# A hybrid attention layer: the stick-breaking mask moves into the running product, keys are stacked by DMA, and top-k steps are spread by other weights

## The chip, the cores and the metric

The kernel runs on one core of a Trainium2 chip. Its engines are TensorE (PE, matmuls, with PEld loading weights), VectorE (DVE), ScalarE (ACT), GpSimd (POOL) and SyncE (SP, which issues all DMA transfers here). The metric is device time in microseconds, the median of several runs; a profile is one execution with the hardware profiler on.

## What is computed

One decoder layer over T = 1040 positions (16 meta tokens and 1024 of the sequence), width 1024. One input projection gives the queries, keys and values of two attention branches, their gates, and an indexer. Cut to what matters here:

```python
# branch a: stick-breaking, 8 heads of 64
z = q @ k.T * 64 ** -0.5
mask = key_pos < q_pos                                   # strictly causal
log_beta = log_sigmoid(z)
log_1m = where(mask, log_beta - z, 0)
suffix = reverse_cumsum(log_1m) - log_1m
a = where(mask, exp(log_beta + suffix), 0);  y_a = a @ v
# branch b: every query attends to the 256 best keys of the indexer
score = where(causal, sum_h(relu(qi_h @ ki.T) * wi_h), -inf)
idx = top_k(score, 256)                                  # ties: the earlier key
y_b = softmax(q @ k[idx].T * 64 ** -0.5 + rel_bias) @ v[idx]
# both: gates, two projections, an output projection, residual, layer norm
```

## The kernel before

The sequence is stored in reverse, so that the suffix sum is a running product from left to right: with 1 - sigmoid(z) = sigmoid(-z), the scan of sigmoid(-z) over the keys gives the products, and differences of the values (dv) replace differences of the products. Products of float matrices are made from a high part and a low part (hi and lo) in three or two matmuls.

Work comes in stages: layer norm and the first projections, the indexer's scores, branch a (about 203 to 691 us), branch b, and the tail with the output projections. Branch a has 32 units: 4 groups m of two heads h, and 4 pairs pr of blocks of 128 queries. Its loop (lines 1081 to 1096) weaves, unit by unit, five generators: `stick_scores` of the next unit (977), `stick_values` of this one (1018), the projections of the next group and the gates (`projections`, 334), and two feeds of top-k steps. PE's instructions are pinned to the order in which they are written; the other engines' order is set by a scheduler that follows program order as far as buffers and its own estimates allow. Operations of the top-k feeds are "behind" (934): they follow the stage's own last operation and nothing of the stage waits for their place.

Scores: `qk` (476) multiplies a block of 128 queries with chunks of the stacked keys, hi and lo of the query; in the first chunk of each of the 8 blocks of a head a third product, of an identity and the tile `not_before`, adds -30000 where a key is not yet allowed. ACT takes sigmoid(-z) into `ct`, DVE scans it in place (989).

Keys: `k_item` (382) projects 128 columns, which are two heads, in three chunks of 348, 346 and 346. Per head, ACT copies 64 rows into rows 0 to 63 of the tile `sk`, and DVE writes what the copy's rounding left out into rows 64 to 127. The projection's PSUM tag `pj` has two banks. For branch b's keys (one head) `extra` copies the values from the same bank, after the keys.

Top-k: for 7 blocks, j = 0 to 6, of width 1040 - 128j, the 256th best score is found bit by bit, 15 steps on the high 16 bits of the scores, 16 on the low ones. DVE does blocks 2 to 6 (`step`, 820: five counts and three small operations), ACT and POOL do blocks 0 and 1 (`act_topk`, 855) with sums of signs into a junk tile with the one-buffer tag `sca`. Between the halves, `low_half` (828) loads the scores again from DRAM, into the one-buffer tag `se`. After the last bit `topk` (914) runs what is left of ACT's steps (920), forms the thresholds of all blocks and calls `select` (894) for each: load the scores into `se`, count, mark the equal ones, rank them by a scan into a tile with tag `sca`, and write the mask through POOL. A generator's `yield` tells its cost to the weaving; here each step counts 1:

```python
    TOPK_OPS = 33 * (NK - len(AB)) + 3 * NK
    ACT_OPS = 34 * len(AB)
    spare = [max(0.5, TK_SLOT - stick_busy(i)) for i in range(TK_END)] + [0.0] * (len(units) - TK_END)
    n_tk = (TOPK_OPS + 1) * spare[i] / sum(spare)
    n_at = ACT_OPS / AT_END
```

DVE's top-k budget is thus spread over the first 30 units, ACT's over the first 26. `keep_y` (950) splits a finished output of a branch into two halves of one tile on POOL and stores both with one transfer.

Of the kernel before, what the change touches and what calls it, by code (L numbers as in the profile page):

```python
# [49 lines left out]
TK_END, TK_SLOT, TK_FILL = 30, 16.0, 3.0  # L50
# [6 lines left out]
AB, AT_END = (0, 1), 26  # L57
# [111 lines left out]
def layer_kernel(ctx: ExitStack, tc: tile.TileContext, x, meta, g_col, b_col, g_row, b_row, rel,  # L169
# [306 lines left out]
    def qk(j, c0, n, q2, sk, mask=None):  # L476
# [4 lines left out]
        if mask is not None:  # L481
            mm(p[:, mask:mask + 128], ident_h, not_before, start=False, stop=False)
# [21 lines left out]
    wsc = cst.tile([128, NB, 8], F32, name="wsc")  # L504
    m9 = cst.tile([128, 9], F32, name="m9")
    v9 = cst.tile([128, 9], F32, name="v9")
# [215 lines left out]
    ski = idxp.tile([128, T], F32R, name="ski")  # L722
    sc = idxp.tile([128, off(NB)], F32, name="sc")
# [104 lines left out]
    def low_half(j):  # L828

        st = sbt([128, T], F32, "se", "st")  # L830
        SY.dma_start(st[:, :width(j)], sc_d[:, span(j)])
        yield 1
        lw = sbt([128, T], U16, "scr", "lw")
        l16 = st.bitcast(U16).rearrange("p (n two) -> p n two", two=2)[:, :width(j), 0]
        V.tensor_scalar(lw[:, :width(j)], l16, sgn[:, j:j + 1], lofs[:, j:j + 1], op0=ALU.mult, op1=ALU.add)
        V.scalar_tensor_tensor(yk[:, span(j)], xk[:, span(j)], top[:, j:j + 1], lw[:, :width(j)],
                               op0=ALU.is_equal, op1=ALU.mult)
# [17 lines left out]
    def act_topk():  # L855
# [5 lines left out]
        def steps(keys, bits):  # L861
            for b in bits:
                for j in AB:
# [5 lines left out]
                    yield 1  # L869
# [6 lines left out]
        for j in AB:  # L876
# [16 lines left out]

    def select(j):
# [11 lines left out]
        yield 1  # L906
# [5 lines left out]
        yield 1  # L912

    def topk():
# [13 lines left out]
        for j in range(NK - 1, -1, -1):  # L928
            yield from select(j)
# [522 lines left out]
```

## Time and profile before

| | us |
|---|---|
| median of 3 runs | 1080.26 (1079.41 to 1080.92) |
| the profiled execution, its own time | 1082.33 |
| its span, first to last instruction | 1079.2 |
| PE / DVE / ACT / POOL busy | 1023.9 / 800.7 / 554.7 / 406.6 |
| mean granted clock of TensorE | 0.983 |

All times in the rows are microseconds from the start of the span unless marked ns. In a row of a timeline the first two numbers are the start and the length; `out<-in` are the program's tile names; a bracket tells the idle time of that engine before the instruction, and what ended it. L218 and L228 are helpers through which all operations of DVE and ACT, and all matmuls, pass. "pj" is a projection's bank, "z" a bank of scores, "atr" and "vtr" transposes, "pv" weighted values, "st" and "s" reloaded scores, "lw" a low half, "scr" the counts' junk output. A row of a stretch has its ends, its length, the busy time of PE, PEld, DVE, ACT and POOL with their instructions, the mean granted clock (1.00 is 2.4 GHz), the DMA engines' share and GB/s. A row of a group ends with its count, busy us, mean ns of one, and the engine's idle time before it; a row of waits with us in total, times and the longest; a row of DMA issues with count, KB each and median us from issue to landing.

### The profile page before, as it was taken

How to read it: one execution, taken by the hardware profiler on the slowest of the kernel's cores; microseconds unless marked ns; L12 is line 12 of the kernel's file. 1: busy time of each engine (PE TensorE's matmuls, PEld its weight loads, DVE VectorE, ACT ScalarE, POOL GpSimd, SP SyncE). 2: the span in 40 equal slices, each digit the busy share in tenths (PEclk: the TensorE clock that was granted, in tenths of full speed). 3: DMA queues.
4: the chain of work that ended last, by engine and by line, in shares of the span. 5: the costliest groups of instructions: out<-in, count | busy, mean ns of one | idle time of the engine just before them, and what ended most of it. 6: DMA issues, size and time to landing. Idle time of an engine off the chain costs nothing.

```text
span 1079.2 us, 16973 instructions
## 1 busy us (share of the span) xinstructions
PE 1023.9 (95%) x5659; PEld 877.5 (81%) x5659; DVE 800.7 (74%) x1721; ACT 554.7 (51%) x1223; POOL 406.6 (38%) x542
## 2 busy tenths in 40 slices
PE   4989999999999998999999989999999999999997
PEld 3878889887888897888888877888888888877886
DVE  7845778787878797878878788277777787277755
ACT  4615566565666555665665343366666765145000
POOL 4312111344354445543544426543535341263000
PEclk8989999999999998999999999999999999999999
DMA  7543655315222433315122534442525853787311
GB/s 278 196 130 89 147 123 157 116 57 152 66 98 84 118 109 105 123 64 137 55 93 94 151 96 131 157 122 82 142 70 130 302 164 127 251 275 258 122 40 58
DMA packets 77255, 142.15 MB, mean 132 GB/s; under 512 B 9400, under 2 KB 28600, under 8 KB 77040
## 3 DMA queue, kind: packets, MB, share of 16 engines
q1 hardware_dynamic: 77168, 141.08, 42.6%
q8 instruction: 44, 0.72, 0.3%
q14 instruction: 43, 0.35, 0.1%
HBM read 78.38 MB, written 39.65 MB: 109 GB/s over the span
## 4 chain that ended last, share of the span: by engine, by line
PE 72%; DVE 14%; DMA 6%; issue 3%; ACT 3%; POOL 1%; SPq 0%; DVEq 0%; ACTq 0%; POOLq 0%
PE pj L228 36%; PE z L228 9%; PE po L228 8%; PE pv L228 7%; PE br L228 5%; PE ptr L231 3%; PE atr L231 3%; DVE scr L218 2%; DMA s<-sc_d 2%; DVE ct L218 2%; DVE hT L218 2%; DVE rank L218 1%; DMA wraw<-in_w_o_dram 1%; DMA st<-sc_d 1%; DVE e L218 1%
## 5 line engine op out<-in xcount | busy, mean ns | idle before, releaser
L228 PE MATMUL pj<-hT,whi 128*128 128x512 f32 (+4 forms) x1680 | 503.8, 382 | 15.7 <-DVE sk L218 6.5
L228 PEld LDWEIGHTS pj<-hT,whi 128*128 128x128 f32 x1680 | 286.5, 193 | 43.3 <-DVE hT L218 7.3
L228 PE MATMUL pj<-hT,wlo 128*128 128x512 f32 (+4 forms) x840 | 312.4, 372 | 0.0
L316 POOL TENSOR_TENSOR wlo<-wraw,whi 128x512 fp32r<-128x512 f32 x108 | 149.0, 1381 | 189.8 <-ACT whi L218 173.3
L228 PEld LDWEIGHTS pj<-hT,wlo 128*128 128x128 f32 x840 | 161.9, 193 | 24.2
L218 DVE TENSOR_SCALAR_CACHE_REDUCE scr<-mk_all,cand 128x784 bf16<-128x784 int16 (+9 forms) x160 | 120.9, 755 | 2.3
L228 PE MATMUL z<-sk,sq 128*128 128x272 f32 (+3 forms) x448 | 120.5, 344 | 1.5 <-ACT ct L218 1.0
L218 ACT ACTIVATE whi<-wraw 128x512 fp32r<-128x512 f32 x108 | 67.8, 629 | 66.4 <-PE pj L228 41.4
L218 DVE TENSOR_TENSOR_SCAN ct<-ct 128x1040 f32<-128x1040 f32 (+3 forms) x64 | 96.4, 1507 | 4.3 <-ACT ct L218 4.1
L228 PEld LDWEIGHTS z<-sk,sq 128*128 128x128 f32 x448 | 78.7, 191 | 12.9 <-DVE mxs L218 2.9
L228 PE MATMUL po<-wo,M 128*128 128x512 f32 (+1 forms) x408 | 88.8, 379 | 0.0
L228 PEld LDWEIGHTS po<-wo,M 128*128 128x128 f32 x408 | 73.3, 188 | 15.6 <-DVE gt L218 0.6
L228 PE MATMUL br<-yh,whi 128*128 128x512 f32 x256 | 82.0, 401 | 2.6 <-DVE gt L218 2.6
L1129 POOL TENSOR_TENSOR mb<-mk_all,nbt 128x256 f32<-128x256 bf16 (+3 forms) x64 | 46.5, 730 | 81.8 <-DVE mxs L218 77.3
L218 ACT ACTIVATE ct<-z 128x272 f32<-128x272 f32 (+3 forms) x112 | 50.4, 452 | 41.9 <-PE z L228 38.4
L218 ACT ACTIVATE sca<-mk_all,ncand 128x1040 bf16<-128x1040 int16 (+1 forms) x64 | 70.8, 1107 | 0.5
L218 DVE TENSOR_TENSOR atlo<-atr,athi 128x512 fp32r<-128x512 f32 x80 | 54.7, 686 | 21.5 <-ACT athi L218 15.9
L866 POOL TENSOR_SCALAR dn<-sg,need 128x1 f32<-128x1 f32 x62 | 23.6, 380 | 122.8 <-ACT sca L218 121.7
L218 DVE SCALAR_TENSOR_TENSOR sc<-r,wsc,sc 128x272 f32<-128x272 f32 (+4 forms) x98 | 57.2, 609 | 14.8 <-ACT r L218 14.0
L218 ACT ACTIVATE r<-z 128x272 f32<-128x272 f32 (+4 forms) x112 | 49.2, 452 | 35.2 <-PE z L228 29.0
L218 ACT ACTIVATE athi<-ptr 128x512 fp32r<-128x512 f32 (+1 forms) x96 | 52.9, 558 | 26.4 <-PE ptr L231 24.8
L218 DVE TENSOR_TENSOR atlo<-ptr,athi 128x512 fp32r<-128x512 f32 (+1 forms) x96 | 61.1, 644 | 6.2 <-ACT athi L218 3.2
(205 smaller groups left out, 1750.1 us busy)
## 6 DMA issues: line engine op xcount, KB each, us to landing
sq<-aq SPq DMA_DIRECT2D x96, 256.0 KB, 4.0
wraw<-in_w_in_dram SPq DMA_DIRECT2D x92, 256.0 KB, 2.9
g_d<-gs SPq DMA_DIRECT2D x34, 256.0 KB, 2.2
gt<-g_d SPq DMA_DIRECT2D x32, 256.0 KB, 3.6
xn_d<-xt SPq DMA_DIRECT2D x8, 512.0 KB, 3.6
xr<-xn_d SPq DMA_DIRECT2D x32, 128.0 KB, 2.3
res_d<-xr SPq DMA_DIRECT2D x32, 128.0 KB, 1.8
ya_d<-yl SPq DMA_DIRECT2D x16, 256.0 KB, 2.8
```

Of the source, the lines that this page charges most:

```text
L218: ins = getattr(self.engine, op)(*args, **kw)
L228: pin(nc.tensor.matmul(*args, **kw))
L231: pin(nc.tensor.transpose(*args))
L316: last_lo[0] = G.tensor_tensor(lo, raw, f(hi), ALU.subtract).ins.name
L866: G.tensor_scalar(dn[:, c], sg[:, c], need2[:, c], -(2.0 ** b), op0=ALU.is_ge, op1=ALU.mult)
L1129: G.tensor_tensor(mb[:, :n], mk[:, :n], NBT[m][:, h, :n], ALU.add)
```

## The change

The mask product and its two constant tiles go. The scan takes a second tensor, `not_yet`, which is 1 where a key is not yet allowed and 0 elsewhere, and keeps the larger of product and mask, so the running product stays 1 up to the first allowed key. With two heads, `k_item` copies all 128 rows into a tile `ak` of the tag `A`, subtracts once, and sends the four quarters to the two `sk` tiles by DMA; `extra` now comes first. The top-k generators yield estimated times in place of 1. `low_half` becomes one generator over several blocks that loads the next block as soon as the present one's low half is extracted. `topk` selects blocks 6 to 2 first, and only then runs the rest of ACT's steps, forms the thresholds of blocks 0 and 1, and selects these. The two budgets are spread over 32 and 28 units. `keep_y` writes the low part in place and stores in two transfers. The tiles `wsc`, `m9`, `v9` move to the indexer's pool.

```diff
-TK_END, TK_SLOT, TK_FILL = 30, 16.0, 3.0
+TK_END, TK_SLOT, TK_FILL = 32, 16.0, 3.0
-AB, AT_END = (0, 1), 26
+AB, AT_END = (0, 1), 28
...
-    ident_h = cst.tile([128, 128], BF16, name="ident_h")
-    V.tensor_copy(ident_h, ident)
-    not_before = cst.tile([128, 128], BF16, name="not_before")
-    V.memset(not_before, -30000.0)
-    G.affine_select(not_before, not_before, [[-1, 128]], ALU.is_ge, 0.0, base=0, channel_multiplier=1)
...
             cs = slice(c0, c0 + n)
+            if extra:
+                extra(ci, c0, n, p)
+            if len(rows) == 2:
+                a = sbt([128, 2, 348], F32R, "A", "ak")
+                A.activation(a[:, 0, :n], p[:, :n], AF.Copy)
+                V.tensor_tensor(a[:, 1, :n], p[:, :n], f(a[:, 0, :n]), ALU.subtract)
+                for t, r in zip(SK[key], rows):
+                    for i in range(2):
+                        SY.dma_start(f(t[64 * i:64 * i + 64, cs]), f(a[r:r + 64, i, :n]))
+                return
             for t, r in zip(SK[key], rows):
                 A.activation(t[0:64, cs], p[r:r + 64, :n], AF.Copy)
                 V.tensor_tensor(t[64:128, cs], p[r:r + 64, :n], f(t[0:64, cs]), ALU.subtract)
-            if extra:
-                extra(ci, c0, n, p)
...
         mm(p[:, :n], q2[:, 0, qs], sk[:, c0:c0 + n], start=True, stop=False)
-        if mask is not None:
-            mm(p[:, mask:mask + 128], ident_h, not_before, start=False, stop=False)
         mm(p[:, :n], q2[:, 1, qs], sk[:, c0:c0 + n], start=False, stop=True)
...
+    LOAD, LW, YK, EQ, RANK = 1.0, 0.0015, 0.002, 0.0017, 0.0031
+    def count_cost(j):
+        return 0.2 + width(j) / 925
...
-            yield 1
+            yield count_cost(j)
...
+    def low_half(blocks):
+        def load(j):
+            st = sbt([128, T], F32, "se", "st")
+            SY.dma_start(st[:, :width(j)], sc_d[:, span(j)])
+            return st
+        st = load(blocks[0])
+        yield LOAD
+        for j, j1 in zip(blocks, blocks[1:] + [None]):
+            lw = sbt([128, T], U16, "scr", "lw")
+            l16 = st.bitcast(U16).rearrange("p (n two) -> p n two", two=2)[:, :width(j), 0]
+            V.tensor_scalar(lw[:, :width(j)], l16, sgn[:, j:j + 1], lofs[:, j:j + 1], op0=ALU.mult, op1=ALU.add)
+            if j1 is not None:
+                st = load(j1)
+            yield LW * width(j)
+            V.scalar_tensor_tensor(yk[:, span(j)], xk[:, span(j)], top[:, j:j + 1], lw[:, :width(j)],
+                                   op0=ALU.is_equal, op1=ALU.mult)
+            yield YK * width(j)
...
-        yield 1
+        yield LOAD
         t_ = f(thr)
         count(s[:, :w], t_, j)
         V.tensor_scalar(cnt[:, j:j + 1], cnt[:, j:j + 1], -float(TOPK), None, op0=ALU.add)
+        yield count_cost(j)
         e = sbt([128, T], I16, "scr", "e")
         r = sbt([128, T], I16, "sca", "rank")
         V.tensor_scalar(e[:, :w], s[:, :w], t_[:, j:j + 1], None, op0=ALU.is_equal)
+        yield EQ * w
         V.tensor_tensor_scan(r[:, :w], e[:, :w], e[:, :w], 0.0, ALU.add, ALU.max)
-        yield 1
+        yield RANK * w
         V.scalar_tensor_tensor(r[:, :w], r[:, :w], cnt[:, j:j + 1], e[:, :w], op0=ALU.is_le, op1=ALU.mult)
+        yield RANK * w
         V.scalar_tensor_tensor(e[:, :w], s[:, :w], t_[:, j:j + 1], r[:, :w], op0=ALU.is_ge, op1=ALU.subtract)
+        yield EQ * w
...
-        run(at.rest())
-        V.tensor_copy(thr, top)
...
+        threshold(vs)
         s = mk_all[:, span(NB - 1)]
         V.memset(s, 0.0)
         causal_mask(s)
-        for j in range(NK - 1, -1, -1):
+        for j in range(NK - 1, len(AB) - 1, -1):
+            yield from select(j)
+        run(at.rest())
+        threshold(slice(0, len(AB)))
+        for j in AB[::-1]:
             yield from select(j)
...
+    TOPK_OPS = (32 * sum(map(count_cost, rest)) + sum(map(count_cost, range(NK))) + (NK + 1) * LOAD
+                + sum((LW + YK) * width(j) for j in rest) + sum(2 * (EQ + RANK) * width(j) for j in range(NK)))
+    ACT_OPS = 32 * sum(map(count_cost, AB)) + LOAD + sum((LW + YK) * width(j) for j in AB)
...
-        G.tensor_copy(t[:, 0], y)
-        G.tensor_tensor(t[:, 1], y, f(t[:, 0]), ALU.subtract)
-        SY.dma_start(dst, f(t))
+        G.tensor_copy(t, y)
+        G.tensor_tensor(y.bitcast(F32R), y, f(t), ALU.subtract)
+        SY.dma_start(dst[:, 0], f(t))
+        SY.dma_start(dst[:, 1], y)
+    not_yet = stkp.tile([128, T], BF16, name="not_yet")
+    V.memset(not_yet, 0.0)
+    V.memset(not_yet[:, 0:128], 1.0)
+    G.affine_select(not_yet[:, 0:128], not_yet[:, 0:128], [[-1, 128]], ALU.is_ge, 0.0, base=0, channel_multiplier=1)
...
-            V.tensor_tensor_scan(b, b, b, 1.0, ALU.mult, ALU.min)
+            V.tensor_tensor_scan(b, b, not_yet[:, :w], 1.0, ALU.mult, ALU.max)
```

## Rows read from the trace of the kernel before

**Rows 1.** The page, busy time of each engine, share, instructions.

```profile
PE 1023.9 (95%) x5659; PEld 877.5 (81%) x5659; DVE 800.7 (74%) x1721; ACT 554.7 (51%) x1223; POOL 406.6 (38%) x542
```

**Rows 2.** Stretches of the stick-breaking stage (columns as told above).

```profile
251.90:301.60 49.70, 45.12 (x278) 41.62 (x276) 38.38 (x78) 29.47 (x67) 22.61 (x34) 0.97 0.35 99
301.60:385.30 83.70, 83.44 (x460) 70.80 (x460) 67.73 (x148) 52.15 (x112) 40.15 (x67) 1.00 0.35 105
385.30:437.00 51.70, 44.60 (x269) 40.36 (x267) 45.11 (x84) 28.35 (x66) 24.67 (x30) 0.93 0.34 100
...
506.80:566.60 59.80, 56.83 (x340) 50.30 (x338) 47.95 (x105) 38.36 (x87) 28.65 (x47) 1.00 0.24 78
566.60:691.00 124.40, 117.95 (x639) 99.45 (x638) 94.11 (x157) 49.91 (x110) 56.90 (x64) 0.99 0.39 117
```

**Rows 3.** Timeline of PE, a masked chunk, then one of the later branch.

```profile
385.16 0.29 PE L228 MATMUL z<-sk,sq 128*128 128x272 f32 x1
...
385.54 0.27 PE L231 MATMUL atr<-ident,ct 128*128 128x128 f32 x1
...
701.74 0.41 PE L228 MATMUL z<-sk,sq 128*128 128x272 f32 x2
701.99 0.27 PE L231 MATMUL pv<-ident,smb 128*128 128x128 f32 x1
```

**Rows 4.** Groups by form on DVE, 190 to 690: two scans.

```profile
L218 DVE TENSOR_TENSOR_SCAN ct<-ct 128x912 f32<-128x912 f32 x8 | 16.4, 2054 | 0.1
...
L218 DVE TENSOR_TENSOR_SCAN rank<-e 128x912 int16<-128x912 int16 x1 | 2.0, 2027 | 0.0
```

**Rows 5.** Timelines of DVE and ACT, one key chunk.

```profile
271.53 0.51 DVE L218 TENSOR_TENSOR sk<-pj,sk 64x348 fp32r<-64x348 f32 x1
272.56 0.52 DVE L218 TENSOR_TENSOR sk<-pj,sk 64x348 fp32r<-64x348 f32 x1 [0.52 <-ACT sk L218]
...
272.08 0.46 ACT L218 ACTIVATE sk<-pj 64x348 fp32r<-64x348 f32 x1 [6.52 <-DVE sk L218]
```

**Rows 6.** Waits of ACT and PE, 190 to 692.

```profile
ACT sk L218 <- DVE sk L218: 24.2, 7, 6.5
ACT vtb L218 <- DVE sk L218: 10.6, 3, 4.2
...
PE pj L228 <- DVE sk L218: 6.5, 6, 2.0
...
PE pj L228 <- ACT vtb L218: 2.5, 1, 2.5
```

**Rows 7.** Groups by form on ACT, 190 to 690: a 128-row copy.

```profile
L218 ACT ACTIVATE kv<-pj 128x348 f32<-128x348 f32 x3 | 1.4, 453 | 0.0
```

**Rows 8.** DMA issues, the queries' transfers.

```profile
sq<-aq SPq DMA_DIRECT2D x96, 256.0 KB, 4.0
```

**Rows 9.** Timelines of SP, DVE, PE at the low halves; one load's issue.

```profile
407.00 8.64 SPq L831 DMA_DIRECT2D st<-sc_d  x3
...
410.83 0.69 DVE L218 TENSOR_SCALAR lw<-st,sgn,lofs 128x784 uint16<-128x784 uint16 x1 [2.75 <-DMA st<-sc_d]
...
423.00 1.11 PE L231 MATMUL vtr<-ident,dv 128*128 128x128 f32 x4 [5.38 <-DVE at L218]
...
st<-sc_d SPq DMA_DIRECT2D x1, 392.0 KB, 3.7
```

**Rows 10.** The page, the group of all counts on DVE.

```profile
L218 DVE TENSOR_SCALAR_CACHE_REDUCE scr<-mk_all,cand 128x784 bf16<-128x784 int16 (+9 forms) x160 | 120.9, 755 | 2.3
```

**Rows 11.** Timeline of DVE, first and last use of rank in two selections.

```profile
633.98 2.32 DVE L218 TENSOR_TENSOR_SCAN rank<-e 128x656 int16<-128x656 int16 x1
...
639.98 0.89 DVE L218 SCALAR_TENSOR_TENSOR e<-s,thr,rank 128x656 int16<-128x656 f32 x1
...
647.13 2.24 DVE L218 TENSOR_TENSOR_SCAN rank<-e 128x784 int16<-128x784 int16 x1
...
650.57 1.30 DVE L218 SCALAR_TENSOR_TENSOR e<-s,thr,rank 128x784 int16<-128x784 f32 x1
```

More of the change, by code (lines that the diff above doesn't have):

```diff
@@ L474, in zb_item, with qk @@
         return Z_B + m, Q_CH, evac, None
-    def qk(j, c0, n, q2, sk, mask=None):
+    def qk(j, c0, n, q2, sk):
         p = pst("z", "z")
@@ L503, in layer_kernel @@
     ki = {}
-    wsc = cst.tile([128, NB, 8], F32, name="wsc")
-    m9 = cst.tile([128, 9], F32, name="m9")
-    v9 = cst.tile([128, 9], F32, name="v9")
     def ki_evac(ci, c0, n, p):
@@ L722, in layer_kernel @@
     ski = idxp.tile([128, T], F32R, name="ski")
+    wsc = idxp.tile([128, NB, 8], F32, name="wsc")
+    m9 = idxp.tile([128, 9], F32, name="m9")
+    v9 = idxp.tile([128, 9], F32, name="v9")
     sc = idxp.tile([128, off(NB)], F32, name="sc")
@@ L826, in step @@
         V.tensor_scalar(cand[:, vs], cand[:, vs], -(2.0 ** (b - 1) if b else 1.0), None, op0=ALU.add)
-    def low_half(j):
-        st = sbt([128, T], F32, "se", "st")
-        SY.dma_start(st[:, :width(j)], sc_d[:, span(j)])
-        yield 1
[L833 to L837, printed above, removed]
+    def low_half(blocks):
[15 more added lines that the diff above has]
+            yield YK * width(j)
     def low_halves():
@@ L843, in low_halves @@
             count(xk[:, span(j)], cand, j)
-            yield 1
+            yield count_cost(j)
         V.tensor_tensor(need[:, vs], need[:, vs], cnt[:, vs], ALU.subtract)
-        for j in range(len(AB), NK):
-            yield from low_half(j)
+        yield from low_half(list(range(len(AB), NK)))
         V.memset(cand[:, vs], float(1 << 15))
@@ L868, in steps @@
                                     op0=ALU.add, op1=ALU.add)
-                    yield 1
+                    yield count_cost(j)
         G.memset(ncand, 0.5 - (1 << 14))
@@ L881, in act_topk @@
             G.tensor_scalar(need2[:, c], need2[:, c], sg[:, c], -float(width(j)), op0=ALU.subtract, op1=ALU.add)
-            yield 1
-        for j in AB:
-            yield from low_half(j)
+            yield count_cost(j)
+        yield from low_half(list(AB))
         G.memset(ncand, 0.5 - (1 << 15))
@@ L892, in causal_mask, with threshold @@
         G.affine_select(s[:, 0:128], s[:, 0:128], [[1, 128]], ALU.is_ge, -BIG, base=0, channel_multiplier=-1)
+    def threshold(c):
+        V.tensor_copy(thr[:, c], top[:, c])
+        V.tensor_copy(thl[:, c], cand[:, c])
+        V.scalar_tensor_tensor(thr[:, c], thr[:, c], 16, thl[:, c], op0=ALU.logical_shift_left, op1=ALU.bitwise_or)
+        V.tensor_tensor(thr[:, c], thr[:, c], rowm[:, c], ALU.bitwise_xor)
     def select(j):
@@ L901, in select @@
         V.tensor_scalar(cnt[:, j:j + 1], cnt[:, j:j + 1], -float(TOPK), None, op0=ALU.add)
+        yield count_cost(j)
         e = sbt([128, T], I16, "scr", "e")
@@ L927, in topk @@
         causal_mask(s)
-        for j in range(NK - 1, -1, -1):
+        for j in range(NK - 1, len(AB) - 1, -1):
             yield from select(j)
-    TOPK_OPS = 33 * (NK - len(AB)) + 3 * NK
-    ACT_OPS = 34 * len(AB)
+        run(at.rest())
+        threshold(slice(0, len(AB)))
+        for j in AB[::-1]:
+            yield from select(j)
+    rest = range(len(AB), NK)
+    TOPK_OPS = (32 * sum(map(count_cost, rest)) + sum(map(count_cost, range(NK))) + (NK + 1) * LOAD
+                + sum((LW + YK) * width(j) for j in rest) + sum(2 * (EQ + RANK) * width(j) for j in range(NK)))
+    ACT_OPS = 32 * sum(map(count_cost, AB)) + LOAD + sum((LW + YK) * width(j) for j in AB)
     def behind(gen):
@@ L983, in stick_scores @@
             for ci, (c0, n, s) in enumerate(key_chunks(j)):
-                z = qk(j, c0, n, SQ[f"a{m}", pr // 2][h], SK[m][h], s if ci == 0 else None)
+                z = qk(j, c0, n, SQ[f"a{m}", pr // 2][h], SK[m][h])
                 o = c0 + s - 128 * j
@@ L1090, in layer_kernel @@
         fill = max(0.0, total / 8 - vc - sc_)
-        n_tk = (TOPK_OPS + 1) * spare[i] / sum(spare)
+        n_tk = (TOPK_OPS + 0.5) * spare[i] / sum(spare)
         residual(i)
@@ L1186, in dsa_values @@
         if m < 3:
-            keep_y(yb_d[m][:, :, cs], y, sbt([128, 2, 512], F32R, "A", "yl"))
+            keep_y(yb_d[m][:, :, cs], y, sbt([128, 512], F32R, "A", "yl"))
             return
```

8 lines of the change are left out of this document (1 added, 7 removed).

## The prediction

> **What bounds the kernel now.** I read the page's busy row first, then the stretches, then the waits of single engines, then the timeline inside the stretches that stick out. The busy row [rows 1] says that TensorE (PE) is busy for 95% of the span and VectorE (DVE) for 74%, and nothing about where the other time goes. The stretches [rows 2] do. A unit of the stick-breaking stage begins where PE starts the next unit's scores. Six undisturbed units take 83.70 us, 13.95 each, with PE never idle to speak of and DVE busy 67.73 us, 11.3 per unit. Other units of the same work take longer: three take 49.70 (7.9 too much), three 51.70 (9.9), four 59.80 (4.0). The last eight carry 432 more rows of projection among them, 24 matmul passes each at the kernel's own 1/2400 us per column, 0.54 us per unit; at 14.5 each their 124.40 us are 8.4 too many. So this stage is bound by PE, and stands about 30 us above that bound. In the two worst stretches the mean granted clock is 0.97 and 0.93: after a long wait PE gets its lower level (1.2 of 2.4 GHz) for some us, and the excess holds that loss too.
>
> **Part 1, the mask.** A masked score chunk is hi product, mask product, lo product. For 272 columns it takes 385.16 to 385.54, 0.38 us; the same chunk without a mask in the later branch takes 701.74 to 701.99, 0.25 us [rows 3]. The mask costs 0.13 us. There are 64 of them (8 heads, 8 blocks), all where PE is the bound: 64 x 0.13 = **8.3 us less**. The bounds are 0 (another engine takes over at once) and 8.3; I take 8.3, as PE hardly idles in undisturbed units. The Trainium skill, TensorE: Matmul & The Clock Gate, Back-to-back issue gap, gives 81 ns per matmul for a stream of 128-column matmuls with their weight loads; by that the term would be 5.2 us and the time 3 us longer. The row decides, because it has the mixed operand types of this sequence.
>
> The mask moves into the scan, which then reads a second tensor in 16-bit form. The scan of floats takes 2054 ns for 912 columns, one that reads and writes 16-bit integers 2027 [rows 4]. I take no change; the bounds are those 27 ns either way for each of 64 scans, 1.7 us of DVE time beside PE. Building the new mask tile (a memset over 1040 columns, one over 128, one selection) falls before the first scan, where PE has projections to go on with; between 0 and 1 us, a scan's time for as many columns halved, taken at 0.3. The three setup operations that go stood beside the first loads: 0.
>
> **Part 2, the keys.** The two heads' rows of a chunk are now copied and subtracted one after the other in one bank: ACT copies head 0, DVE subtracts at 271.53, only then does ACT copy head 1 at 272.08, and DVE subtracts at 272.56 [rows 5]. ACT stands still for 6.5 us, and the projection's bank comes free 1.0 us later than one subtraction would free it. Over the stage ACT waits 24.2 us for these subtractions and 10.6 for the value half of the last such item; PE waits 6.5 and 2.5 us for the same bank [rows 6]. After the change there is one ACT copy of all rows (453 ns for 128 rows [rows 7], against 0.46 us for 64 [rows 5]) and one subtraction, and ACT no longer waits for DVE between them; in the last item ACT's copy goes first. Twelve copies of 0.45 us leave ACT and twelve subtractions of 0.51 us leave DVE, 6 us of DVE in four places. Of the stretch excess I give this part 4.0 of the 7.9 (what stays there is the wait for a gate and a slow scan), 2.5 of the 4.0, and 2.0 of the last 8.4.
>
> What it adds: 48 transfers of 87 KB on SP's queue. The nearest row is the queries' 64-row transfers of 256 KB, 4.0 us to landing [rows 8]. The keys of the later groups are first read more than two units (28 us) after their projection, so 4 us are hidden; those of the first group are read soon after, with the values' projection between: bounds 0 and 4 us. If SP is held while it waits for a subtraction (up to 6.5 us, as above), weight loads, gate stores and residual rows queue behind it; weights are fetched one item ahead, some 7 us, which is the cover. With the cover gone it is up to 4 us per group, 16 in all. For all of this I take 0.5, as the queries' transfers, which are larger, go the same way now. The shared double buffer now also holds a chunk until its transfers land; values that follow may start late by part of 4 us, on POOL, taken at 0.5 in all. The branch outputs written as two transfers (22 more) have no reader until the next stage: 0.
>
> **Part 3, the top-k steps.** At 407 three loads of low halves go through one buffer in a row; DVE sits 2.75 us for one of them, and PE then waits 5.38 us for a transpose's bank [rows 9]. The changed order issues the next load before the second operation of the present block, and puts (0.0015 + 0.002) x width, 2.7 of its cost units for 784 columns, between loads. At 191 units over 32 slots, 6.0 each, that is 0.45 of a slot, 6 us, more than the 3.7 us of such a load. That is most of the 9.9 us: I take 7.0, the key copies in that stretch included.
>
> The selections: the old plan gives 21 of 187 steps to seven blocks, 3.4 slots, and DVE is overfull there. The new weights give five blocks 34.2 of 191, 5.7 slots, and the last two 23.2, 3.9 slots. I take 3.0 of the last stretch's 8.4, beside the 2.0 above. Together the stretches give back 4.0 + 7.0 + 2.5 + 5.0 = **18.5 us**.
>
> The price is paid earlier. Fifteen steps of five counts had 12.0 slots, 6.2 counts per slot; a step now weighs 3.85, so they have 15 x 3.85/6.0 = 9.7 slots, 7.7 counts. A count is 755 ns [rows 10]: 1.1 us more DVE per slot, and up to 1.4 with the small operations between steps, which I set at a quarter of that at most. From 11.3 in 13.95 it goes to 12.4 to 12.7 in 13.7. Bounds: 0, and about 0.6 us in each of 22 slots; I take **3 us**. Then the rank tile of a selection and the junk output of ACT's counts share one buffer ("sca"), and only now do both run at once: bounds 0 and rival 2's price, taken at **2 us**. The thresholds of the last two blocks must wait for ACT's last count, whose budget ends in the same slot: about 0.2. With the 0.3, 0.5 and 0.5 above, **1.5 us**.
>
> **The sum.** 8.3 + 18.5 - 3 - 2 - 1.5 = 20.3 us less. Against the profiled execution's 1082.3 this is 1062.0; that execution is 2.1 above the median of the runs, so I predict **1060.0**. About 0.2% (2.2 us) is what a measurement of this kernel can tell from no change.
>
> **Rivals.** *1. DVE becomes the bound in the first 22 slots.* For: 91 to 93% of a slot is more than any undisturbed stretch shows. Against: its work is spread evenly and PE runs two groups ahead. Price: 0.6 x 22 = 13 us in place of 3, so 1070.
>
> *2. The shared buffer turns the selections into waits (slower).* Rank is held from the scan to the last use: 4.7 us for 784 columns (647.13 to 651.87) and 6.9 for 656 (633.98 to 640.87) [rows 11], 8.1 ns per column, 21.3 us for the 2640 columns of five blocks. If ACT's next count is queued in order behind each hold, scores and transposes behind it stop too; with a fall to the lower clock at each (1.5 us lost, 0.03 of 49.70 as in the stretch with 0.97) it costs 28.8 in place of 2: 1086.8. It decides from 22 us of such loss. Against: the counts run behind the stage's own work, which may pass them.
>
> *3. The key change does not do what it says.* The subtraction at 271.53 was late because scans and counts stood before it, not because of the second head. Then only the last hop of 1.0 us per chunk goes, and some 2.5 of the 8.5 us that I give the keys remain: 1066.
>
> *4. All of it goes.* The excess falls by 26 and nothing new appears: 1080.3 - 8.3 - 26 = 1046; half the way there from the forecast is 1053.
>
> **How the numbers follow.** Forecast 0.60 (own range 1053 to 1067), rival 1 0.14, rival 2 0.07, rival 3 0.11, rival 4 0.08. The range 1050 to 1076 leaves out rival 2, the far end of rival 1 and half of rival 4. Slower: rival 2 and a little of rival 1, 0.09; within 0.2%: 0.04; faster: 0.87.
>
> **What would show it.** Right: no mask products, two-product chunks of 0.25 us; no wait of ACT for a key subtraction; PE's wait at the low halves below 1 us; undisturbed units near 13.7; PE's two waits for the keys' bank [rows 6] under 3 us together. Wrong: DVE gaps vanish in the first 22 units while PE waits for "atlo"; ACT waits for "rank" or DVE for "sca"; the lower clock granted in the selections.

## The result, and the profile after

The changed kernel takes 1061.67 us (median; 1060.51 to 1063.28), the kernel before 1080.34 on the same chip: 18.7 us less, a ratio of 0.9829 (95% interval 0.9812 to 0.9846). The profiled execution took 1062.54, its span is 1060.8.

The page's busy row of the changed kernel, which answers to [rows 1]:

```profile
PE 1013.7 (96%) x5595; PEld 876.5 (83%) x5595; DVE 791.8 (75%) x1713; ACT 550.6 (52%) x1211; POOL 420.4 (40%) x542
```

The 64 mask products are gone (5659 to 5595), and DVE has 8.9 us less to do. The stretches, as in [rows 2]: units 3 to 5, unit 6 (undisturbed before, and there part of the longer row of units 6 to 11), units 12 to 14, 20 to 23, and 24 to the end of the stage.

```profile
252.10:296.20 44.10, 42.10 (x269) 39.81 (x268) 38.48 (x81) 26.93 (x61) 22.99 (x30) 1.00 0.49 132
296.20:315.50 19.30, 16.52 (x76) 13.71 (x75) 15.01 (x39) 10.21 (x25) 8.05 (x14) 0.82 0.19 65
383.90:432.90 49.00, 42.92 (x263) 39.62 (x262) 43.47 (x91) 23.39 (x57) 21.27 (x26) 0.97 0.41 114
501.40:559.20 57.80, 55.69 (x331) 50.12 (x331) 49.89 (x109) 37.84 (x85) 33.76 (x49) 1.00 0.35 104
559.20:674.00 114.80, 113.45 (x624) 97.86 (x623) 76.08 (x102) 58.07 (x125) 66.32 (x78) 1.00 0.41 124
```

Units 3 to 5 and the last eight became shorter by the most; units 12 to 14 still hold a stall (clock 0.97), and unit 6 has a new one, with a mean granted clock of 0.82. The waits of PE between 190 and 675 us (total, times, longest), which answer to [rows 6]:

```profile
PE vtr L231 <- DVE at L218: 8.3, 3, 4.1
PE pj L228 <- DVE ak L218: 2.4, 2, 1.6
PE atr L231 <- DVE cand L218: 2.0, 1, 2.0
PE pj L228 <- DVE sk L218: 1.2, 1, 1.2
PE pj L228 <- DVE aq L218: 0.4, 1, 0.4
PE z L228 <- ACT ct L218: 0.3, 1, 0.3
```

The waits for the keys' bank fell from 9.0 to 3.6 us. The longest that are left are three waits of the values' transposes (vtr) for `at`, the small DVE subtraction at a unit's start. Those of ACT in the same time:

```profile
ACT sca L218 <- DVE e L218: 7.7, 4, 4.4
...
ACT ak L218 <- DMA sq<-aq: 3.1, 2, 2.2
...
ACT ak L218 <- DVE ak L218: 1.9, 1, 1.9
```

The 24.2 us behind the first head's subtraction are gone. The shared buffer does make ACT wait (7.7), but PE waits for ACT only 0.3 us in the whole stage, and from 559 us on, where the selections are, its only wait is one of 1.2 us for a key subtraction (`sk`). So no time was lost there.

How far the changed kernel is ahead, by the start of the same PE instruction in both traces (before, after), with the forecast's terms put into the same stretches (mask at 0.26 us per unit):

| up to | before | after | gained in the stretch | forecast |
|---|---|---|---|---|
| start of unit 0 | 210.6 | 211.7 | -1.1 | 0 |
| unit 3 | 251.8 | 252.1 | 0.8 | 0.8 |
| unit 6 | 301.4 | 296.2 | 5.5 | 4.8 |
| unit 12 | 385.2 | 383.9 | **-3.9** | 1.6 |
| unit 15 | 436.9 | 432.9 | **2.7** | 7.8 |
| unit 20 | 506.6 | 501.4 | 1.3 | 1.3 |
| unit 24 | 566.5 | 559.2 | 2.0 | 3.5 |
| branch b | 702.8 | 686.0 | 9.5 | 7.1 |
| end | 1079.2 | 1060.8 | 1.6 | 0 |

The forecast's gains in this column are 26.9 us; it has 6.5 of debits besides, which it did not divide among these stretches.

### The profile page after: what moved, and what is told of

It reads as the page before. It is cut to its first block, busy times and chain, and to the rows that moved or that the text cites. A ratio compares the mean times of both kernels' runs of the same rounds, so it can differ in the third digit from the quotient of the medians.

```text
span 1060.8 us, 17034 instructions
## 1 busy us (share of the span) xinstructions
PE 1013.7 (96%) x5595; PEld 876.5 (83%) x5595; DVE 791.8 (75%) x1713; ACT 550.6 (52%) x1211; POOL 420.4 (40%) x542
## 4 chain that ended last, share of the span: by engine, by line
PE 68%; DVE 14%; DMA 9%; issue 3%; ACT 3%; POOL 2%; SPq 1%; DVEq 0%; ACTq 0%; POOLq 0%
PE pj L228 34%; PE po L228 8%; PE z L228 8%; PE pv L228 7%; PE br L228 4%; PE ptr L231 3%; DVE scr L218 3%; PE atr L231 2%; DMA sq<-aq 2%; DVE hT L218 2%; DMA wraw<-in_w_o_dram 2%; DVE ct L218 1%; DVE atlo L218 1%; DMA wraw<-in_w_in_dram 1%; POOL xr L1006 1%
## 5 line engine op out<-in xcount | busy, mean ns | idle before, releaser
L311 POOL TENSOR_TENSOR wlo<-wraw,whi 128x512 fp32r<-128x512 f32 x108 | 151.7, 1406 | 223.8 <-ACT whi L218 212.5
L228 PE MATMUL z<-sk,sq 128*128 128x272 f32 (+3 forms) x448 | 112.2, 332 | 0.8 <-ACT ct L218 0.3
L218 DVE TENSOR_TENSOR_SCAN ct<-ct,not_yet 128x1040 f32<-128x1040 f32 (+3 forms) x64 | 96.4, 1507 | 5.9 <-ACT ct L218 5.8
L228 PEld LDWEIGHTS z<-sk,sq 128*128 128x128 f32 x448 | 76.6, 189 | 13.6 <-DVE mxs L218 2.8
L218 DVE SCALAR_TENSOR_TENSOR sc<-r,wsc,sc 128x272 f32<-128x272 f32 (+4 forms) x98 | 57.8, 618 | 14.6 <-ACT r L218 14.0
L218 DVE TENSOR_TENSOR atlo<-atr,athi 128x512 fp32r<-128x512 f32 x80 | 54.2, 684 | 18.3 <-ACT athi L218 14.9
L218 ACT ACTIVATE athi<-atr 128x512 fp32r<-128x512 f32 x80 | 47.4, 597 | 24.8 <-PE atr L231 23.6
```

Source lines behind the costliest of these rows:

```text
L218: ins = getattr(self.engine, op)(*args, **kw)
L228: pin(nc.tensor.matmul(*args, **kw))
L311: last_lo[0] = G.tensor_tensor(lo, raw, f(hi), ALU.subtract).ins.name
```

## Experiments

Each kernel ran beside the kernel before on the same chip. The table gives the length of the units in the profiled executions (from the first scores product that PE makes in a unit to that of the next); "30, 31" is the stretch of the last two together. Of the units left out, 2, 13, 16, 17 and 21 move by 1 to 2 us in some runs; the rest are undisturbed.

| unit | before | after | e1 | e2 | e3 | e4 | e6 | e5 | e8 | e9 |
|---|---|---|---|---|---|---|---|---|---|---|
| 3 | 17.0 | 14.8 | 18.1 | 14.5 | 16.9 | 14.2 | 15.4 | 14.0 | 17.5 | 13.9 |
| 4 | 17.9 | 15.8 | 15.9 | 17.0 | 14.9 | 15.3 | 15.7 | 15.2 | 16.0 | 15.1 |
| 5 | 14.7 | 13.6 | 13.9 | 14.7 | 13.6 | 13.6 | 13.6 | 13.6 | 13.6 | 13.6 |
| 6 | 14.1 | **19.2** | 15.3 | 15.1 | 14.0 | 15.9 | 17.5 | 14.0 | 14.0 | 14.0 |
| 12 | 15.1 | 16.0 | 17.1 | 18.3 | 13.9 | 18.9 | 18.9 | **19.7** | 13.9 | 14.2 |
| 14 | 21.5 | **19.4** | 18.3 | 19.2 | 19.9 | 19.3 | 17.7 | 14.0 | 14.0 | 14.0 |
| 20 | 15.2 | 14.0 | 14.1 | 16.0 | 14.0 | 15.1 | 14.0 | 14.5 | 17.2 | 16.4 |
| 22 | 14.8 | 15.0 | 15.2 | 15.5 | 14.6 | **19.1** | 15.1 | 13.7 | 14.0 | 14.0 |
| 27 | 18.0 | 16.1 | 15.5 | 16.4 | 17.9 | 17.5 | 16.0 | 16.7 | 17.7 | 16.9 |
| 28 | 16.4 | 14.2 | 14.5 | 14.2 | 15.8 | 14.9 | 14.3 | 15.3 | 14.6 | 14.2 |
| 29 | 16.5 | 14.5 | 14.6 | 14.4 | 15.8 | 14.4 | 14.7 | 14.4 | 14.4 | 14.4 |
| 30, 31 | 31.6 | 29.0 | 29.1 | 29.0 | 33.3 | 29.0 | 29.0 | 29.0 | 29.0 | 29.0 |

### One part undone in the changed kernel

**e1: the mask product back**, with its constants; the scan as before.

```diff
+        if mask is not None:
+            mm(p[:, mask:mask + 128], ident_h, not_before, start=False, stop=False)
...
-            V.tensor_tensor_scan(b, b, not_yet[:, :w], 1.0, ALU.mult, ALU.max)
+            V.tensor_tensor_scan(b, b, b, 1.0, ALU.mult, ALU.min)
```

> The kernel after the change, with the mask product, its two constants and the old scan put back; all else stays. My theory (the product costs 0.13 us on the engine that bounds the stage, 64 times): 8.3 us over the changed kernel, about 1070.0, and undisturbed units 0.26 us longer, 13.9 in place of 13.65. Rival (in the changed kernel VectorE is near the bound, so PE's freed time is worth half at most): 1066 or less. Rival (the order on VectorE, which the scheduler draws up anew for every program, moves more than the product does): the undisturbed units are 0.26 us longer, but the sum differs from 8.3 by more than 4 us through waits in other units.

Measured: 1066.66 us, ratio 0.9878 (0.9864 to 0.9893), 0.0049 or 5.3 us above the changed kernel. Undisturbed units take 0.21 to 0.27 more, two masks of 0.13, as forecast. The total lies between the theory's 1070 and the first rival's 1066, because other units move as well: 3 and 12 take 3.4 and 1.1 more, 6 and 14 take 4.0 and 1.1 less.

**e2: the keys back to two copies and two subtractions.**

```diff
-            if len(rows) == 2:
-                a = sbt([128, 2, 348], F32R, "A", "ak")
...
-                return
```

> The changed kernel with the old key item: two ACT copies and two subtractions of 64 rows per chunk, in turn, no DMA for the keys. My theory (ACT's waits for the subtractions held the projection's bank and ACT's queue): 4 to 9 us slower, 1066 to 1071, ACT waits for sk of some 24 us come back, and PE's waits for this bank go from 3.6 us to 6 or more. Rival (the subtractions were late because of other work ahead of them on VectorE, and only the last hop of 1 us per chunk went): 1 to 3 us slower, 1063 to 1065.

Measured: 1068.77 us, ratio 0.9897 (0.9881 to 0.9914), 7.3 us above. ACT's waits in this kernel:

```profile
ACT sk L218 <- DVE sk L218: 25.1, 8, 6.9
...
ACT vtb L218 <- DVE sk L218: 4.3, 2, 2.9
```

They are back, and with them 1.2, 1.1, 2.3 and 2.0 us in units 4, 5, 12 and 20; PE's waits for the keys' bank are 6.6 us, and 1.7 for the value copy, in place of 3.6. The theory holds. Unit 6 again takes 4.1 less.

**e3: the old plan of the top-k steps**: each step counts 1, the budgets go over 30 and 26 units, a low half is loaded when the one before is done, and all selections come after ACT's steps.

```diff
-TK_END, TK_SLOT, TK_FILL = 32, 16.0, 3.0
+TK_END, TK_SLOT, TK_FILL = 30, 16.0, 3.0
-AB, AT_END = (0, 1), 28
+AB, AT_END = (0, 1), 26
...
-            yield count_cost(j)
+            yield 1
```

> The changed kernel with the whole old top-k plan: every step counts 1, the old loads of low halves, all blocks selected after ACT's steps are done, 30 and 26 units. My theory (the overfull selections cost some 6 us in units 27 to 30, and the new plan's dense counts give 5 us of that back in unit 6): 1 to 6 us slower, 1063 to 1068; units 27 to 30 take 2 us each more, unit 6 takes 14 in place of 19.2. Rival (the new weights are worth what I forecast, 10 us less what I set against them, 5): 1066 to 1068 with unit 14 at 21.5 again. Rival (they are worth nothing): 1060 to 1063.

Measured: 1067.62 us, ratio 0.9890 (0.9875 to 0.9905), 6.6 us above. Units 27 to 29 take 4.6 more, 30 and 31 another 4.4, and 3 takes 2.2 more. Unit 6 has no stall at all (14.0), and 12 is undisturbed (13.9). Unit 14 stalls under this plan too (19.9), with other work ahead of `at`: here it is low halves (DVE stands 1.53 us for a load at 409.21), in the changed kernel counts, as shown further down.

### One part alone on the kernel before

**The mask change** (with the tile moves, and `keep_y` in two transfers, that make room for its tile; the same lines the other way round). No run takes `keep_y` by itself.

```diff
-            mm(p[:, mask:mask + 128], ident_h, not_before, start=False, stop=False)
...
+            V.tensor_tensor_scan(b, b, not_yet[:, :w], 1.0, ALU.mult, ALU.max)
```

> The kernel before with the mask change alone (and the tile moves that make room for the mask tile). Theory: 0.26 us per undisturbed unit, 8 us over 32 units, and DVE's order at the start of unit 6 is still that of the kernel before, so that no new stall comes: 1070 to 1074 against 1080. Rival: the waits of PE on DVE in the disturbed units take up what the mask products leave, so that only the 17 undisturbed units gain, 4.4 us: 1075 to 1077.

Measured: 1076.90 us, ratio 0.9974 (0.9961 to 0.9987): 3.4 us less by the medians, 2.8 by the ratio, in the rival's 1075 to 1077. Seventeen units of this stage are undisturbed both before and after; 17 x 0.26 is 4.4. Units 3 to 5, 12, 13 and 20 to 22 stay within 0.25 of their length before: there PE ends up at the same wait for DVE, and comes to it earlier. The other units moved both ways in the profiled execution (14 and 29 take 2.0 and 1.9 less, 28 takes 2.5 and 30 and 31 take 4.8 more), and that execution, 1080.39, is the longest of the ten, so this account by units is shown for some of them only.

**The key change:**

```diff
+                A.activation(a[:, 0, :n], p[:, :n], AF.Copy)
+                V.tensor_tensor(a[:, 1, :n], p[:, :n], f(a[:, 0, :n]), ALU.subtract)
+                for t, r in zip(SK[key], rows):
+                    for i in range(2):
+                        SY.dma_start(f(t[64 * i:64 * i + 64, cs]), f(a[r:r + 64, i, :n]))
+                return
```

> The kernel before with the key change alone. Theory: units 3 to 5, 12 and 20 to 22 lose what the changed kernel gained there by the keys, 6 to 8 us, and no new stall comes: 1072 to 1075. Rival, the last subtraction was late because of other work on DVE: 2 us or less, 1078 to 1080.

Measured: 1073.77 us, ratio 0.9930 (0.9912 to 0.9948): 6.6 us less by the medians, 7.6 by the ratio; the theory holds. No new stall in unit 6 (14.1), and 12 is undisturbed (14.1).

**The top-k plan:**

```diff
-            yield 1
+            yield count_cost(j)
...
-        for j in range(NK - 1, -1, -1):
+        for j in range(NK - 1, len(AB) - 1, -1):
             yield from select(j)
```

> The kernel before with the new plan of the top-k steps alone (and the tile moves): mask products and keys as before. Theory: the last units (27 on) gain 5 to 8 us as the five selections have more room, but the denser steps put counts ahead of the small subtraction at the start of unit 6, which then takes over 17 us (14.07 before), and unit 14 keeps its 20 us: 1073 to 1078. Rival, the stall of unit 6 needs all three parts together: unit 6 under 15, 1070 to 1073. Second rival, the plan gives nothing: 1079 to 1082.

Measured: 1074.59 us, ratio 0.9949 (0.9933 to 0.9966): 5.0 us less by the medians, 5.5 by the ratio, in the theory's range. What the theory said of unit 6 was wrong: 15.2 us, 1.2 more than before and no full stall. The last units gain 7.5 (5.0 in 27 to 29, 2.5 in 30 and 31), unit 12 loses 3.3 (18.4), unit 14 keeps 19.5.

So the three parts alone give 3.4 + 6.6 + 5.0 = 15.0 (by the ratios 2.8 + 7.6 + 5.5 = 15.9), undone, by the ratios, 5.3 + 7.3 + 6.6 = 19.2, together 18.7. The sums agree within what the intervals allow (1 to 2 us for each part alone, some 2.5 for each undone), though single stalls do not add up so: that of unit 6 comes in full only with all three.

### What the stalls of units 6, 14 and 22 wait for

In the changed kernel, DVE at the start of unit 6, and at 413 to 420 that of unit 14:

```profile
297.09 1.21 DVE L218 SCALAR_TENSOR_TENSOR cand<-hit,cand 128x5 f32<-128x5 f32 x1
298.33 0.69 DVE L218 TENSOR_SCALAR cand<-cand 128x5 f32<-128x5 f32 x1
299.06 1.03 DVE L218 TENSOR_SCALAR_CACHE_REDUCE scr<-mk_all,cand 128x784 bf16<-128x784 int16 x1
...
300.01 0.72 DVE L218 TENSOR_TENSOR_SCAN ct<-ct,not_yet 128x272 f32<-128x272 f32 x1
300.76 0.29 DVE L218 TENSOR_TENSOR at<-atr,at 128x128 fp32r<-128x128 f32 x1
...
413.17 0.16 DVE L218 SCALAR_TENSOR_TENSOR cand<-hit,cand 128x5 f32<-128x5 f32 x1
...
417.52 0.49 DVE L218 TENSOR_SCALAR_CACHE_REDUCE scr<-mk_all,cand 128x272 bf16<-128x272 uint16 x1
...
417.94 1.48 DVE L218 TENSOR_TENSOR_SCAN ct<-ct,not_yet 128x272 f32<-128x272 f32 x1
419.45 0.29 DVE L218 TENSOR_TENSOR at<-atr,at 128x128 fp32r<-128x128 f32 x1
```

and PE in the same kernel:

```profile
301.11 1.12 PE L231 MATMUL vtr<-ident,dv 128*128 128x128 f32 x4 [2.79 <-DVE at L218]
...
419.80 1.13 PE L231 MATMUL vtr<-ident,dv 128*128 128x128 f32 x4 [4.13 <-DVE at L218]
```

`at` needs 0.29 us, but in unit 6 a bit step's end, a count and a scan stand before it, and in unit 14 five counts (413.57 to 418.0, the last is shown) and the scan. Until it is done it holds one of three transpose banks, which the second group of value transposes wants. Units 6, 14 and 22 are those in which the next group's values are transposed. In unit 14 this is the stall of [rows 9]: the low halves of blocks 2 to 6 lie in units 10 to 12 now, and it stayed.

**e4: next to no top-k budget in units 6, 14 and 22.**

```diff
+    for i in (6, 14, 22):
+        spare[i] = 0.5
```

> The changed kernel with nearly no top-k budget for VectorE in units 6, 14 and 22, in which PE transposes the next group's values; the steps go to the other units, 0.5 us more VectorE time in each. My theory (PE waits 3 to 4 us there for the third transpose bank, since counts stand ahead of the small subtraction that frees it, and the low clock follows): units 6, 14 and 22 take about 14 us each, 10 us less in all, and some 2 us come back elsewhere: 1052 to 1056. Rival (the bank is late for another reason, ACT or the values themselves): units 6 and 14 stay above 17 us, 1060 to 1064.

Measured: 1068.97 us, ratio 0.9903 (0.9887 to 0.9920), 8 us slower than the changed kernel: the theory fell. Unit 14 stays at 19.3 and unit 22 rises to 19.1. The next theory was that the steps ahead of `at` are those given to the unit *before*; those units got their share of what was taken away. In unit 6 the same wait was a little shorter, and only that; PE, and the stretch of that unit:

```profile
299.38 0.65 PE L231 MATMUL vtr<-ident,dv 128*128 128x128 f32 x4 [2.32 <-DVE at L218]
```

```profile
295.00:310.80 15.80, 13.48 (x75) 11.30 (x74) 8.13 (x19) 9.81 (x25) 7.52 (x14) 1.00 0.22 70
```

After 2.32 us of waiting the clock stayed at 1.00, and the unit is 1.9 longer than without a stall (14.0); after 2.79 in the changed kernel the mean over 19.3 us was 0.82, and the unit is 5.2 longer. So about half of that stall (5.2 less the 2.79 of waiting, an estimate) is the lower of the two clock levels.

**e6: another bank for the small transpose**, and nothing else: DVE's order is that of the changed kernel.

```diff
-            p = pst("tr", "atr")
+            p = pst("z" if (h, pr) == (1, 2) and m < 3 else "tr", "atr")
             tp(p[:, 0:128], ct[:, 0:128], ident)
```

> The changed kernel, the order of all engines' work as it is, but the first small transpose of units 6, 14 and 22 goes into a bank of scores ('z') in place of one of the three banks for transposes, so that a value transpose no longer waits for 'at'. Theory A, only the bank stops PE and DVE catches up behind PE's projections: the waits of the value transposes for 'at' (8.3 us in three) go, and units 6 and 14 lose 3 us or more each, the lower clock with them: 1051 to 1057. Rival D, DVE itself is late for whatever PE needs next: the same wait comes back at the next transpose or at the scores' bank, under 2 us gained in all: 1059 to 1062.

Measured: 1063.44 us, ratio 0.9838 (0.9819 to 0.9858): nothing gained in all, rival D (1.4 above its range). Units 6 and 14 do take 1.7 less each, but unit 12 takes 2.9 more (PE waits 3.3 us there for `cand` in place of 2.0). The waits of the value transposes for `at` are gone, and PE waits at the next thing that is late:

```profile
298.86 0.55 PE L231 MATMUL vtr<-ident,dv 128*128 128x128 f32 x3 [0.62 <-POOL dv L431]
...
301.86 1.12 PE L231 MATMUL atr<-ident,ct 128*128 128x128 f32 x4 [1.76 <-DVE atlo L218]
...
419.50 0.55 PE L231 MATMUL vtr<-ident,dv 128*128 128x128 f32 x3 [2.56 <-POOL dv L431]
```

POOL, in the same kernel, was late because of DVE as well:

```profile
416.36 0.73 POOL L1091 TENSOR_TENSOR ys<-ys,sil 128x256 f32<-128x256 f32 x1 [2.76 <-DVE ys L218]
417.05 1.26 POOL L311 TENSOR_TENSOR wlo<-wraw,whi 128x512 fp32r<-128x512 f32 x1
418.27 1.18 POOL L431 TENSOR_TENSOR dv<-kv 128x346 f32<-128x346 f32 x1
```

The bank is where the stall shows; most of it comes from DVE's queue.

**e5: next to no top-k budget in the units before**, 5, 13 and 21.

```diff
+    for i in (5, 13, 21):
+        spare[i] = 0.5
```

> The changed kernel with the top-k budget of units 5, 13 and 21 cut to half a cost unit each (the previous run cut that of units 6, 14 and 22), so that their share goes to the other units. Theory A, steps given to the unit before stand ahead of the small subtraction 'at' on DVE, and PE's third value transpose waits for the bank that 'at' frees: units 6, 14 and 22 (19.21, 19.37, 15.04 us in the changed kernel, 13.65 undisturbed) fall to under 15 each, 10 to 12 us less there, and up to 5 us come back in denser units: 1050 to 1057 us against 1061. Rival B, steps that are moved only stall PE elsewhere: 1060 to 1066. Rival C, the stall of unit 14 is that of the low-half loads: unit 14 stays at 18 us or more while 6 falls.

Measured: 1053.83 us (1050.41 to 1056.05), ratio 0.9740 (0.9719 to 0.9760), 9.6 us (0.0089; 7.8 by the medians) better than the changed kernel. Units 6, 14 and 22 take 14.0, 14.0 and 13.7: theory A. The three runs that follow keep this cut, and in all of them these units take 14.0, while in the runs without it unit 14 is never under 17.7. One stall came in unit 12 (19.7). SP, DVE and PE there:

```profile
373.87 3.48 SPq L373 DMA_DIRECT2D sq<-aq  x4
377.44 1.10 SPq L839 DMA_DIRECT2D st<-sc_d  x1
378.58 2.80 SPq L391 DMA_DIRECT2D sk<-ak  x4
```

```profile
382.66 0.42 DVE L218 TENSOR_SCALAR lw<-st,sgn,lofs 128x272 uint16<-128x272 uint16 x1 [4.49 <-DMA st<-sc_d]
...
384.61 0.28 DVE L218 TENSOR_TENSOR at<-atr,at 128x128 fp32r<-128x128 f32 x1
```

```profile
384.95 0.87 PE L231 MATMUL atr<-ident,ct 128*128 128x128 f32 x4 [4.09 <-DVE at L218]
```

The last load of a low half could be issued when its buffer came free at 374.91, but stood behind four query transfers, went out at 377.44, and landed 5.2 us later. DVE stood for it with `at` queued behind. The changed kernel has the same thing more mildly (DVE stands 3.64 us for the load, PE has the 2.0 us for `cand` among its waits, unit 12 is at 16.0).

The key transfers are not what makes this load late. e2 has none, and there the same load stands behind the same query transfers, lands as late (381.23 to 386.47), and unit 12 takes 18.3:

```profile
378.10 3.03 SPq L373 DMA_DIRECT2D sq<-aq  x4
381.23 6.02 SPq L831 DMA_DIRECT2D st<-sc_d  x2
...
386.47 0.42 DVE L218 TENSOR_SCALAR lw<-st,sgn,lofs 128x272 uint16<-128x272 uint16 x1 [2.90 <-DMA st<-sc_d]
```

The top-k plan alone has none either (3.35 us of DVE, unit 12 at 18.4), while the two runs with key transfers and the old plan, the key change alone and e3, leave unit 12 undisturbed. The stall of unit 12 belongs to the place where the new plan puts the low halves.

### Moving the low halves away from the transfers

**e7: the first 11 units get 12% more**, on top of e5.

```diff
+    for i in range(11):
+        spare[i] *= 1.12
```

> The changed kernel with the top-k budget of units 5, 13 and 21 cut (as in the earlier run that took 1053.8 us) and that of the first 11 units raised by 12%, so that the low halves end in unit 11, before the keys of the next group are stacked by DMA. In the run without it DVE stood 4.5 us for a load of low halves that SP had issued behind four query transfers and among key transfers, and unit 12 took 19.72 us (14.1 undisturbed). Theory: away from these transfers the loads are there in time, unit 12 takes under 15.5, 4 to 5 us less: 1047 to 1051. Rival, the denser first units stall PE for as much: 1053 to 1058, with unit 12 low and units 1 to 10 high. Second rival, the loads are late wherever they are, since there is one buffer for them: unit 10 or 11 takes 3 us or more longer in place of unit 12, 1052 to 1056.

Measured: 1059.35 us, ratio 0.9817 (0.9796 to 0.9838): nearest to the first rival, 1.4 above its range. Unit 12 fell only to 17.0, and units 2, 3 and 4 grew from 13.1, 14.0 and 15.2 to 15.1, 16.8 and 18.0.

**e8: unit 11 cut as well**, on top of e5, so that the last two low halves come after `at` of unit 12.

```diff
+    spare[11] = 0.5
```

> The changed kernel with the top-k budget of units 5, 13 and 21 cut, and that of unit 11 too, so that the last two low halves come after the first key transfers in unit 12, behind the small subtraction that the transposes wait for. Theory: the load has a scan and more of the stage's work to hide behind, unit 12 takes 14 to 16 us: 1048 to 1052. Rival, key transfers on SP hold the loads for as long there: unit 12 or 13 takes 18 us or more, 1053 to 1058.

Measured: 1058.90 us, ratio 0.9810 (0.9787 to 0.9832): unit 12 is undisturbed (13.9), as the theory had it, so the rival's reason does not hold; but the total is 0.9 above even the rival's range: what was taken from unit 11 came back in units 2, 3 (15.0, 17.5) and 20 (17.2).

**e9: on top of e5, half of unit 11's budget and a fifth of that of 20, 27 and 28 go to units that no run showed disturbed.**

```diff
+    for i in (5, 13, 21):
+        spare[i] = 0.5
+    freed, spare[11] = 0.5 * spare[11] - 0, 0.5 * spare[11]
+    spare[12] += 0
+    for i in (20, 27, 28):
+        freed += 0.2 * spare[i]
+        spare[i] *= 0.8
+    calm = (15, 16, 17, 18, 19, 23, 24, 25, 26)
+    for i in calm:
+        spare[i] += freed / len(calm)
```

> The changed kernel with the top-k budget of units 5, 13 and 21 cut as in the run of 1053.8 us (so that units 0 to 10 keep that run's budgets), that of unit 11 halved, that of units 20, 27 and 28 cut by a fifth, and what this frees given to units 15 to 19 and 23 to 26, which no run so far showed disturbed at the budgets of the changed kernel. Theory: stalls come where a step stands ahead of something that PE awaits at once, not from the amount of top-k work, so calm units can take more: units 2 to 4 stay at 13.1, 14.0 and 15.2 us, unit 12 falls from 19.72 to under 15.5, units 27 and 28 fall by 1 or more, the calm ones stay within 0.5: 1047 to 1052. Rival, VectorE's work has no room left anywhere: the calm units grow by 3 us or more in all, 1053 to 1057.

Measured: 1053.97 us (1053.23 to 1054.09), ratio 0.9764 (0.9745 to 0.9783). The low halves are solved without a price in the first units (unit 12 at 14.2, units 2 to 4 as in e5), but units 16 and 17 grew by 1.5 and 1.4, unit 20 to 16.4, and the rival's total is met. The stretch of unit 16 in the changed kernel, then those of 16 and 20 in e9:

```profile
447.10:460.70 13.60, 13.60 (x80) 11.88 (x79) 12.92 (x25) 9.14 (x20) 7.54 (x10) 1.00 0.41 118
...
432.50:447.70 15.20, 14.21 (x81) 11.71 (x79) 15.03 (x27) 9.20 (x20) 8.31 (x11) 1.00 0.36 106
...
489.70:506.10 16.40, 14.33 (x99) 13.67 (x99) 16.11 (x37) 9.13 (x20) 7.14 (x8) 1.00 0.55 140
```

DVE is busy for 12.92 of 13.60 us in the first, with PE never idle, and for 15.03 of 15.20 and 16.11 of 16.40 in the others: it has no room left there. PE's longest waits in this kernel:

```profile
PE pj L228 <- DVE ak L218: 2.7, 3, 1.4
PE atr L231 <- DVE at L218: 1.8, 2, 1.1
PE pj L228 <- DVE sk L218: 1.2, 1, 1.2
```

No wait is longer than 1.4 us. e5 and e9 both beat the changed kernel by 7 to 10 us (the intervals do not overlap); which of the two is better these runs do not tell.

## Why the prediction was right, and where not

The forecast of 1060.0 was 1.7 us off, and the range held. Its sum of 20.3 against 18.7 measured is closer than its terms are, and that is luck, as the last paragraph of this section shows.

- **Mask, 8.3: about twice too much.** The row was right (0.38 us per chunk before, 0.26 now, and 0.26 less per undisturbed unit); PE in the changed kernel, the same chunk as in [rows 3]:

```profile
383.90 0.42 PE L228 MATMUL z<-sk,sq 128*128 128x272 f32 x2
384.16 0.27 PE L231 MATMUL atr<-ident,ct 128*128 128x128 f32 x1
```

  The step that failed is "64 x 0.13, as PE hardly idles in undisturbed units": only 17 units are undisturbed. In most of the others the saved time runs into the wait for DVE. Net about 3 alone, 5.3 undone.
- **Scan with a mask tile, 0: right.** 64 scans, mean 1507 ns, in both kernels.
- **Keys, 8.5 less a debit of 1.0: right.** 6.6 alone and 7.3 undone. Rival 3 (2.5 us) is out: the copies' wait for the first subtraction was the cause.
- **SP's debit, 0.5 for the key transfers: no run contradicts it.** What did wait on SP's queue is a load of a low half, and behind the queries' transfers: 2.0 us of PE's waiting in unit 12 of the changed kernel, and in e5 that unit is 5.8 longer than undisturbed (19.7 against 13.9). It comes with the new place of the low halves, with or without key transfers, and no term of the sum had it.
- **Low halves, 7.0 of 9.9: the step that failed most.** It read the 5.38 us of [rows 9] as the end of a chain from the loads, which it was in the kernel before, and took it that the stall goes with them. The bank's holder `at` is late because of whatever top-k work stands before it, loads or counts. With the loads two units away unit 14 stayed at 19.4 us (4.13 of waiting); only emptying the unit before it ended it (e5). The three units gained 2.7 with the mask, in place of 7.8.
- **Selections, 3.0 and 2.0: too small.** The last eight units gained 9.5, of which the masks have at most 2.1; 7.4 or more were to be 5.0.
- **DVE denser in the first 22 slots, 3: right engine, wrong shape.** It came not as 0.14 in each slot but as one stall of 5.2 in unit 6, about half of it the clock. Rival 1, as a general bound at 1070, did not come: units 7 to 11 stayed undisturbed.
- **Shared buffer, 2: nothing.** ACT waits 7.7 us for this buffer, as rival 2 had it, but PE waits for ACT 0.3 us in the whole stage.
- **The rest, 1.5:** the stage began 1.1 us later, and the tail was 1.6 shorter. The 1.1 is no more than profiled executions differ: with the same work ahead of it, unit 0 begins at 211.7 in the changed kernel, 211.2 in e5 and 210.4 in e7. What shortened the tail stays open.

Of the signs that were named, undisturbed units came near 13.7 (13.65), two-product chunks at 0.26, ACT's waits for the key subtractions fell to 1.9 us in one, and the selections kept the full clock (1.00). The waits for the keys' bank came to 3.6 in place of under 3, and PE's wait in unit 14 stayed far above 1. Of the signs of being wrong, ACT's waits for the shared buffer came, and cost nothing.

By stretches the gains fall short of the forecast's 26.9 by 8.5: 5.5 in units 6 to 11, 5.1 in 12 to 14, 1.5 in 20 to 23 and 1.1 at the start, against 0.7, 2.4 and 1.6 more in units 3 to 5, in the last eight and in the tail. The debits of 6.5 had been set for other things (a DVE denser everywhere, the shared buffer), and stood in for this by their size. The total was closer than the reasons.

## What to carry to other kernels

A saving on the bound engine counts only in the stretches where it never waits; elsewhere it becomes a longer wait, so count undisturbed units before multiplying. A stall ends with the last instruction of the queue it waits on, so ask what stands *ahead* of the awaited instruction, and not which slow thing is near: here a 0.29 us subtraction behind other work stopped TensorE for 2.8 and 4.1 us, and did so again when the loads ahead of it had been moved away. When background work is spread over a schedule, take it from the unit ahead of the sensitive point, and expect it to come back where the engine is already full.

## What the hardware showed that was not expected

A DVE instruction on 128x5 numbers took 1.21 us at 297.09 and 0.16 at 413.17 (both above). POOL in the changed kernel, at the first of these times:

```profile
296.99 1.28 POOL L311 TENSOR_TENSOR wlo<-wraw,whi 128x512 fp32r<-128x512 f32 x1
298.23 0.76 POOL L431 TENSOR_TENSOR dv<-kv 128x346 f32<-128x346 f32 x1
```

The DVE instruction ended at 298.30, just after POOL's at 298.27, and the next small one (298.33, 0.69 us) at 299.02, just after POOL's at 298.99. The second takes 0.17 at 413.37. The 1.6 us that the two lost are more than half of the wait that made unit 6 stall. It is no accident of one place: in all traces of this case the first form, begun while a TENSOR_TENSOR of POOL ran, ended 16 to 26 ns after it, 100 times of 100, and the second form 22 to 35 ns after it, 70 of 70; begun with POOL idle they took at most 0.17 us (557 times). The Trainium skill, SBUF — State Buffer, "SBUF: two separate sides", says that VectorE and GpSimd share one pair of ports, which whoever starts first holds for its whole instruction, when VectorE reads two inputs from SBUF (beside a GpSimd instruction that reads SBUF); the traces agree for the first form (two inputs). The second has one tensor input; that it waits too may be the page's other case, a mode of VectorE that uses both ports, and no run here tells whether it is.

Four query transfers of 64 rows each held SP for 3.48 us (e5, at 373.87), 0.87 each, and four key transfers for 2.80 (at 378.58), 0.70 each. What SP issues next goes out that much later: the load whose buffer was free at 374.91 went out at 377.44.
